# Three projection tiles behind the input loads, and the sum of squares split before the first eviction

## The chip, the cores and the metric

The kernel runs on one core of a Trainium2 chip. The metric is the device time of one execution in microseconds, the median of the runs. The engines are TensorE (PE, its weight loads PEld), VectorE (DVE), ScalarE (ACT) and GpSimd (POOL); SyncE (SP) issues nearly all loads, ScalarE's queue a few.

## The reference, cut to what matters

Two layers of a hybrid encoder work on 512 grid tokens and 16 meta tokens (528 columns) of width 1024. A layer takes an RMS norm of its input, one wide projection, global attention (GQA) on one part and windowed attention (NA) on another, gates both, merges them and adds an output projection.

```python
def hybrid_layer(x, norm_g, w_in, q_norm_g, k_norm_g, rpb, w_o_attn, w_o_na, w_out, cos, sin):
    h = rms_norm(x, norm_g)
    proj = jnp.einsum('bld,de->ble', h, w_in)
    qa, ka, va, za, qb, kb, vb, zb, ga, gb = split_cols(proj)
    qa = apply_axial_rope(rms_norm(qa.reshape(...), q_norm_g), cos, sin)
    ka = apply_axial_rope(rms_norm(ka.reshape(...), k_norm_g), cos, sin)
    oa = gqa_attention(qa, ka, va) * jax.nn.silu(za)
    ...
    mixed = jax.nn.sigmoid(ga) * ya + jax.nn.sigmoid(gb) * yb
    return x + jnp.einsum('bld,de->ble', mixed, w_out)
```

## The kernel before, in words

The input comes transposed, in eight feature tiles of 128 features x 528 tokens (264 KB each). A projection tile is 128 columns of w_in; layer 0 starts with QA to QA+3 (queries of the global attention), KA, VA, and then four times KB, QB, VB, ZB, ZA, followed by the gates GB and GA with the output halves y between them. A tile sums over eight k steps. For precision each operand is a high part (fp32r, made by ScalarE) and a low part (the difference, made by VectorE for the input, `normed`, and by GpSimd for the weights), and each k takes three products, for two token halves of 264 columns: 48 matmuls for a tile. The norm's gain is in the operands; the factor of each token (`rbc`) is applied when a later tile is evicted, and the per-head norm of q and k makes the first tiles independent of it.

**The head.** `piece` loads, casts and splits a quarter of the weights of QA or QA+1 (256 columns, two k), `half` a half (512 columns, four k), `feature` one feature tile. The tuple at line 403 sets their order; `in_order` queues each behind the last cast on ScalarE and GpSimd. Behind the last feature tile come the squares of three feature tiles and their adds, the weights of QA+2, and the rest of the squares, some of them behind the first evictions (`input_squares`, `sum_up`, `late`). The products of QA and QA+1 (line 429) follow the feature tiles: QA's sums lie in two banks of the pool `ps_p`, which all later tiles use too, those of QA+1 in the two banks of `S`. QA+2 is the first tile that `product` makes, with `weights` loading and splitting its halves in the list `order`.

**Evictions.** `rotated` empties each half of a tile with three ScalarE instructions (lines 470 to 472) and takes a low part on VectorE; `rotate` are four VectorE instructions, `stack_pair` makes the operand of the attention.

**Side work.** Each half of a `product` ends in a tick. Two queues, `side_gqa` and `side_na`, issue their due parts at ticks: `later(n, part)` is due n ticks on. The sum of the squares is split (`norm_split`), turned into factors (`norm_root`) and spread (`norm_spread`) at the ticks of `NORM_AT`. Attention units start at ticks whose count is a multiple of four (GQA) or one more (NA) and issue scores, transposes and sums some ticks on; `side_na.finish()` and `side_gqa.finish()` tick what is left, behind the third GB and the third GA tile. The products at line 434 have no ticks.

The scheduler orders each engine's instructions by priority (`high_priority`) and by when their inputs and buffers come free in its own reckoning; `issue_after` fixes an order on one engine. The slots of a tag are reused: "O" has 8, "K" 4, "E" 6, "G" 8.

Of the kernel before, what the change touches and what calls it, by code (L numbers as in the profile page):

```python
# [11 lines left out]
F32 = mybir.dt.float32  # L12
F32R = mybir.dt.float32r
I32 = mybir.dt.int32
AF = mybir.ActivationFunctionType
# [23 lines left out]
NA_AT = ({"stages": (0, 2, 5, 5, 5, 7), "values": (3, 4)},  # L39
         {"stages": (0, 2, 4, 5, 5, 7), "values": (3, 4)})  # L40

NORM_AT = ({"tokens": (1, 4, 6), "squares": (2, 2, 2, 3, 2), "heads": (2, 3, 5, 7, 6), "values": (1, 4)},
           {"tokens": (1, 3, 5), "squares": (2, 2, 2, 3, 2), "heads": (2, 3, 5, 7, 6), "values": (1, 4)})
GQA_AT_TICK, NA_AT_TICK = (0, 0), (1, 1)

# [50 lines left out]
def trunk_kernel(ctx: ExitStack, tc: tile.TileContext, xT, w, gn, gf, bias, rope, out):  # L96
# [28 lines left out]
    def bank(pool, name, tag):  # L125
        return pool.tile([P, 512], F32, tag=tag, name=name)
# [81 lines left out]
    for l in range(DEPTH):  # L208
        cols = [QA, QA + 1, QA + 2, QA + 3, KA, VA]
        for j in range(4):  # L210
            cols += [KB + j, QB + j, VB + j, ZB + j, ZA + j]
        order += [(l, c, i) for c in cols for i in range(2)]
        if l == 0:

            order = order[1:2] + order[3:]
        for gate, wo in ((GB, WOB), (GA, WOA)):
            for m in range(8 + LAG):
                order += [(l, gate + m, 0), (l, gate + m, 1)] if m < 8 else []
                order += [(l, wo + (m - LAG) // 2, (m - LAG) % 2)] if m >= LAG else []
        order += [(l, WOUT + m, i) for m in range(8) for i in range(2)] if l < DEPTH - 1 else []  # L220
# [107 lines left out]

    h_last = {}

    def normed(l, k, x, n):

        hi, lo = slot("h", f"hh{l}_{k}", F32R), slot("h", f"hl{l}_{k}", F32R)
        h_last["hi"] = nc.scalar.mul(hi[:, :n], x, g_in[l][:, k:k + 1])
        h_last["lo"] = nc.vector.scalar_tensor_tensor(lo[:, :n], x, g_in[l][:, k:k + 1], hi[:, :n].bitcast(F32),
                                                      op0=ALU.mult, op1=ALU.subtract)
        return hi, lo

    def squared(first, x, n, name):
        sq = slot("R" if first else "G", f"sq{name}")  # L340
        h_last["square"] = nc.scalar.activation(sq[:, :n], x, AF.Square)
        return sq
# [30 lines left out]


    pieces, xs, h, done = {}, [], [], [None, None]

    def in_order(part):
        with ExitStack() as held:
            for ins in done:
                if ins is not None:  # L380
                    held.enter_context(tc.issue_after(ins))
            part()

    def piece(c, i):
        raw = slot("K", f"rawp{c}_{i}")[:, :2 * P]
        hi, lo = (slot("O", f"w{'hl'[v]}p{c}_{i}", F32R)[:, :2 * P] for v in range(2))
        nc.sync.dma_start(raw, w[0, c][:, 2 * P * i:2 * P * (i + 1)])
        done[0] = nc.scalar.copy(hi, raw).ins
        done[1] = nc.gpsimd.tensor_sub(lo, raw, hi.bitcast(F32)).ins
        pieces[c, i] = hi, lo  # L390

    def half(c):
        weights(0, c, 1, 1)
        done[:] = split_at["weights"]

    def feature(k):
        if k % 2 == 0:
            xs.extend(two("M", f"x0_{k}"))
        nc.sync.dma_start(xs[k], xT[k])
        h.append(normed(0, k, xs[k], NTOK))  # L400
        done[0] = h_last["hi"].ins

    for part in ((piece, QA, 0), (feature, 0), (piece, QA + 1, 0), (feature, 1), (piece, QA, 1), (piece, QA + 1, 1),
                 (feature, 2), (feature, 3), (half, QA), (feature, 4), (half, QA + 1), (feature, 5), (feature, 6), (feature, 7)):
        in_order(lambda: part[0](*part[1:]))

    def input_squares(ks):
        return [squared(k == 0, xs[k], NTOK, f"0_{k}") for k in ks]

    def sum_up(sqs):  # L410
        for sq in sqs:
            nc.vector.tensor_add(total["ss"], total["ss"], sq)

    total, late = {}, []
    with tc.issue_after(h_last["hi"].ins), tc.issue_after(h_last["lo"].ins):
        total["ss"], *sqs = input_squares(range(3))
        sum_up(sqs)
    with tc.issue_after(h_last["square"].ins):
        weights(0, QA + 2, 1, 1)
    with tc.issue_after(split_at["weights"][0]):  # L420
        sum_up(input_squares((3, 4)))
        late.append(input_squares((5, 6)))


    first, ends = {}, ((0, HALF), (HALF, NTOK))
    for c, ps in ((QA, [bank(ps_p, f"pp0_{QA}_{a}", "pp")[:, :HALF] for a, _ in ends]),
                  (QA + 1, ps_s.tile([P, 2, 512], F32, tag="S", name=f"pp0_{QA + 1}"))):
        first[c] = [(ps[i] if c == QA else ps[:, i, :HALF], a, b) for i, (a, b) in enumerate(ends)]
    for c, k in sorted(((c, k) for c in first for k in range(KT)), key=lambda x: (x[1] + 2 * (x[0] > QA and x[1] > 3), x[0])):
        wh, wl = (t[:, P * (k % 4):P * (k % 4 + 1)] for t in weights(0, c, k // 4, 1)) if k > 3 else (  # L430
            t[:, P * (k % 2):P * (k % 2 + 1)] for t in pieces[c, k // 2])
        for wt, rt in ((wh, 0), (wh, 1), (wl, 0)):
            for ps, a, b in first[c]:
                nc.tensor.matmul(ps, wt, h[k][rt][:, a:b], start=k == 0 and wt is wh and rt == 0,
                                 stop=k == KT - 1 and wt is wl)

    for l in range(DEPTH):
        last = l == DEPTH - 1
# [21 lines left out]
        def rotated(c, g, full, name):  # L460

            n, j = NTOK if full else NREAL, c - QA

            if name == "k":
                keys.append(slot("KR", f"{name}{l}_{c}")[:, :NTOK + NMETA])
            q = slot("E", f"{name}{l}_{c}") if name == "q" else keys[0][:, NMETA:]
            sq = slot("G", f"{name}s{l}_{c}")
            qh, ql = slot("G", f"{name}h{l}_{c}", F32R), slot("G", f"{name}l{l}_{c}", F32R)
            for ps, a, b in project(c, full):
                nc.scalar.mul(q[:, a:b], ps, g)  # L470
                nc.scalar.activation(qh[:, a:b], ps, AF.Square)
                evac["last"] = nc.scalar.activation(sq[:, a:b], ps, AF.Square)  # L472
            with tc.high_priority():
                evac["low"] = nc.vector.tensor_sub(ql[:, :n], sq[:, :n], qh[:, :n].bitcast(F32))
            side_gqa.later(NORM_AT[l]["squares"][j], lambda: sum_squares(j, n, qh, ql))

            def rotate():
                sh = slot("G", f"{name}r{l}_{c}")
                nc.vector.stream_shuffle(sh[:, :n], q[:, :n], [(i + 16) % 32 for i in range(32)])
                nc.vector.tensor_mul(sh[:, :n], sh[:, :n], sin[:, :n])  # L480
                nc.vector.tensor_mul(q[:, :n], q[:, :n], cos[:, :n])
                nc.vector.tensor_add(q[:, :n], q[:, :n], sh[:, :n])

            return q, rotate
# [56 lines left out]
        st = {}  # L541

        def norm_split():
            st["ss"] = split_squares(total["ss"], NTOK, f"{l}")

        def norm_root():
            st["mx"], st["rx"], st["root"] = inverse_rms(st["ss"], NTOK, f"{l}")
# [24 lines left out]
        for j in range(4):  # L572
            q, rotate = rotated(QA + j, g_q[l], full, "q")
            qs.append(q)

            with tc.issue_after(evac["low"].ins):
                if l == 0 and j < 2:
                    sum_up(late[j])
                if l == 0 and j == 0:
                    turn = rotate  # L580
                    with tc.issue_after(evac["last"].ins):
                        late.append(input_squares((7,)))
                else:
                    if turn:
                        turn()
                    turn = None
                    rotate()
            if j > 1:
                stack_pair(j - 2)
            if j == 0:  # L590
                for after, part in zip(NORM_AT[l]["tokens"], (norm_split, norm_root, norm_spread)):
                    side_gqa.later(after, part)
                if full:
                    side_gqa.later(5, meta_columns)
        k, rotate = rotated(KA, g_k[l], True, "k")
        rotate()
        stack_pair(2)

        def pair_factors(t, c, n, name):

# [123 lines left out]

        v = scaled(VA, f"va{l}")
        with tc.issue_after(evac["v"].ins):
            stack_pair(3)
# [496 lines left out]
```

## Time and profile before

| what | us |
|---|---|
| median of 3 runs | 862.96 |
| lowest, highest | 862.93, 865.67 |
| profiled execution | 862.94 |
| its span, first to last instruction | 861.2 |
| TensorE busy | 849.1 |
| VectorE busy | 533.4 |
| ScalarE busy | 491.6 |
| GpSimd busy | 360.6 |

The span is what the profiler records of the core; the rest of the execution's time lies around it. Busy times are sums of records. Matmuls are pipelined, so their records overlap and short idle times of TensorE don't show in its busy time.

### The profile page before, as it was taken

How to read it: one execution, taken by the hardware profiler on the slowest of the kernel's cores; microseconds unless marked ns; L12 is line 12 of the kernel's file. 1: busy time of each engine (PE TensorE's matmuls, PEld its weight loads, DVE VectorE, ACT ScalarE, POOL GpSimd, SP SyncE). 2: the span in 40 equal slices, each digit the busy share in tenths (PEclk: the TensorE clock that was granted, in tenths of full speed). 3: DMA queues.
4: the chain of work that ended last, by engine and by line, in shares of the span. 5: the costliest groups of instructions: out<-in, count | busy, mean ns of one | idle time of the engine just before them, and what ended most of it. 6: DMA issues, size and time to landing. Idle time of an engine off the chain costs nothing. (4 is left out here: it accounts for less than half of the span.)

```text
span 861.2 us, 16238 instructions
## 1 busy us (share of the span) xinstructions
PE 849.1 (99%) x5960; PEld 788.7 (92%) x5960; DVE 533.4 (62%) x1309; ACT 491.6 (57%) x1178; POOL 360.6 (42%) x287
## 2 busy tenths in 40 slices
PE   8999999999999999999999999999999999999997
PEld 8999999999999999999998999999988888878786
DVE  6985767677774574436548656677767645444633
ACT  8644677576874564333445456578667655543422
POOL 5574233342232333454764653324333233334751
PEclk9999999999999999999999999999999999999999
DMA  6364344325112222325655664334532222223602
GB/s 237 104 190 132 98 118 113 115 64 163 50 50 75 74 74 63 104 84 155 150 137 130 171 172 136 103 98 131 146 103 74 75 75 78 93 79 98 206 22 98
DMA packets 64670, 95.55 MB, mean 111 GB/s; under 512 B 22864, under 2 KB 23376, under 8 KB 64592
## 3 DMA queue, kind: packets, MB, share of 16 engines
q1 hardware_dynamic: 63872, 93.46, 37.2%
q8 instruction: 47, 0.77, 0.4%
q10 hardware_dynamic: 720, 1.06, 0.3%
q14 instruction: 31, 0.25, 0.1%
HBM read 76.72 MB, written 4.19 MB: 94 GB/s over the span
## 5 line engine op out<-in xcount | busy, mean ns | idle before, releaser
L238 POOL TENSOR_TENSOR wlo<-raw,whi 128x512 fp32r<-128x512 f32 x214 | 285.2, 1337 | 453.0 <-ACT whi L237 377.5
L320 PE MATMUL pp<-hh,whi 128*128 128x264 f32 (+1 forms) x1056 | 334.8, 317 | 0.6 <-ACT qs L472 0.6
L322 PE MATMUL pp<-hh,wlo 128*128 128x264 f32 (+1 forms) x1056 | 329.3, 312 | 0.0
L321 PE MATMUL pp<-hl,whi 128*128 128x264 f32 (+1 forms) x1056 | 327.9, 310 | 0.0
L237 ACT CAST whi<-raw 128x512 fp32r<-128x512 f32 x214 | 131.4, 619 | 154.0 <-PE pp L321 57.4
L322 PEld LDWEIGHTS pp<-hh,wlo 128*128 128x128 f32 x1056 | 198.7, 188 | 10.8
L320 PEld LDWEIGHTS pp<-hh,whi 128*128 128x128 f32 x1056 | 198.8, 188 | 10.1 <-ACT qs L472 1.2
L321 PEld LDWEIGHTS pp<-hl,whi 128*128 128x128 f32 x1056 | 199.2, 189 | 9.1
L783 DVE CUSTOM_DVE_ANT_1 P<-S,r 128x528 f32<-128x528 f32 x64 | 45.1, 705 | 19.1 <-PE S L537 18.0
L194 DVE TENSOR_TENSOR ptl<-pt,pth 128x512 fp32r<-128x512 f32 x64 | 44.0, 689 | 17.5 <-ACT pth L193 16.9
L1048 DVE TENSOR_TENSOR mg<-pp,rbc 128x264 f32<-128x264 f32 (+1 forms) x48 | 24.8, 517 | 41.8 <-PE pp L322 41.4
L787 ACT ACTIVATE P<-P,st 128x528 f32<-128x528 f32 x64 | 47.2, 737 | 2.0
L908 ACT ACTIVATE bias<-bias,stb 128x208 f32<-128x208 f32 (+1 forms) x64 | 31.1, 486 | 24.1 <-DVE stb L906 23.8
L129 PE MATMUL pt<-ident,P 128*128 128x128 f32 x256 | 39.4, 275 | 1.3 <-DVE P L789 0.9
L193 ACT CAST pth<-pt 128x512 fp32r<-128x512 f32 x64 | 37.3, 584 | 4.3 <-PE pt L129 3.1
L1049 ACT ACTIVATE mg<-mg 128x264 f32<-128x264 f32 (+1 forms) x48 | 23.7, 493 | 25.9 <-DVE mg L1048 25.8
L321 PE MATMUL pp<-mx,whi 128*128 128x264 f32 x128 | 36.6, 286 | 0.0
L320 PE MATMUL pp<-mx,whi 128*128 128x264 f32 x128 | 36.4, 285 | 0.0
L322 PE MATMUL pp<-mx,wlo 128*128 128x264 f32 x128 | 36.3, 284 | 0.0
L830 PE MATMUL av<-pth,VA 128*128 128x256 f32 x128 | 35.3, 298 | 0.1
L789 DVE TENSOR_SCALAR P<-P,st 128x528 f32<-128x528 f32 x64 | 33.0, 516 | 2.1
L830 PE MATMUL av<-ptl,VA 128*128 128x256 f32 x128 | 33.0, 280 | 0.0
(529 smaller groups left out, 1749.3 us busy)
## 6 DMA issues: line engine op xcount, KB each, us to landing
raw<-in_w_dram SPq DMA_DIRECT2D x214, 256.0 KB, 2.7
bias<-in_bias_dram SPq DMA_DIRECT2D x16, 480.0 KB, 3.8
KB<-KB SPq DMA_DIRECT2D x24, 272.0 KB, 3.8
rawl<-in_w_dram SPq DMA_DIRECT2D x16, 256.0 KB, 3.0
x<-in_xT_dram SPq DMA_DIRECT2D x8, 264.0 KB, 4.3
xr<-in_xT_dram SPq DMA_DIRECT2D x8, 264.0 KB, 4.1
Q<-q SPq DMA_DIRECT2D x16, 128.0 KB, 3.2
x1d<-xt SPq DMA_DIRECT2D x32, 64.0 KB, 2.8
```

The costliest lines, as they stand in the source:

```text
L129: nc.tensor.transpose(ps, src, ident[:n, :n])
L193: split_at["hi"] = nc.scalar.copy(hi, src)
L194: split_at["any"] = nc.vector.tensor_sub(lo, src, hi.bitcast(F32))
L237: cast = nc.scalar.copy(hi, raw)
L238: sub = nc.gpsimd.tensor_sub(lo, raw, hi.bitcast(F32))
L320: nc.tensor.matmul(ps, wh, rh[:, a:b], start=i == 0, stop=False)
L321: nc.tensor.matmul(ps, wh, rl[:, a:b], start=False, stop=False)
L322: nc.tensor.matmul(ps, wl, rh[:, a:b], start=False, stop=i == n - 1)
L783: newest["max"] = nc.vector.tensor_tensor_reduce(p[:n].rearrange("p (i k) -> p i k", i=2), S[:n, :, :HALF], scale[:n].unsqueeze(2).to_broa ...
L787: nc.scalar.activation(p[:n], p[:n], AF.Exp, bias=st[:n, 1:2], scale=1.0, accum_out=st[:n, 2:3])
L789: nc.vector.tensor_scalar_mul(p[:n], p[:n], st[:n, 3:4])
L830: nc.tensor.matmul(c["av"], rows2(c["t"][i][0]), c["t"][i][1], start=i == 0, stop=i == 8)
```

## The change

Three tiles, QA, QA+1 and QA+2, follow the input. Their weights lie in memory as eight row tiles: row tile k holds the 384 columns of all three tiles for one k (192 KB). The head loads a row tile and a feature tile in turn. From k = 4 on the square of feature tile k - 4 and its add are put behind feature tile k; the other four, the first half of QA+3's weights and the split of the sum follow. The first feature tile's high part is made in two halves. QA+2's sums lie in the banks `avn` and `avg`, which the attention uses later. The products of k = 0 to 3 go through all three tiles, the later ones in a written order that ends QA first. Each half's evictions are queued behind the ones before. Numbers of ticks in `NORM_AT` and the places of `stack_pair` are edited, and `order` begins with QA+3.

```diff
-NORM_AT = ({"tokens": (1, 4, 6), "squares": (2, 2, 2, 3, 2), "heads": (2, 3, 5, 7, 6), "values": (1, 4)},
+NORM_AT = ({"tokens": (1, 1, 3), "squares": (1, 1, 2, 3, 2), "heads": (2, 3, 5, 7, 6), "values": (1, 4)},
...
-            order = order[1:2] + order[3:]
+            order = order[6:]
...
+    w3 = w[0, QA:QA + 3].rearrange("c p n -> (c p n)").rearrange("(k p n) -> k p n", k=KT, p=P)
...
-    def piece(c, i):
-        raw = slot("K", f"rawp{c}_{i}")[:, :2 * P]
-        hi, lo = (slot("O", f"w{'hl'[v]}p{c}_{i}", F32R)[:, :2 * P] for v in range(2))
-        nc.sync.dma_start(raw, w[0, c][:, 2 * P * i:2 * P * (i + 1)])
+    def row_tile(k):
+        raw = slot("K" if k < 4 else "E", f"rawp{k}")[:, :3 * P]
+        in_turn(raw, w3[k])
+        hi, lo = (slot("O", f"w{'hl'[v]}p{k}", F32R)[:, :3 * P] for v in range(2))
         done[0] = nc.scalar.copy(hi, raw).ins
         done[1] = nc.gpsimd.tensor_sub(lo, raw, hi.bitcast(F32)).ins
-        pieces[c, i] = hi, lo
+        pieces[k] = hi, lo
...
     def feature(k):
...
-        nc.sync.dma_start(xs[k], xT[k])
-        h.append(normed(0, k, xs[k], NTOK))
+        in_turn(xs[k], xT[k])
+        h.append(normed(0, k, xs[k], NTOK, ((0, HALF), (HALF, NTOK)) if k == 0 else None))
         done[0] = h_last["hi"].ins
...
+    def add_up(k):
+        sq = square(k)
+        if k == 0:
+            total["ss"] = sq
+        else:
             nc.vector.tensor_add(total["ss"], total["ss"], sq)
...
+    def next_weights():
+        weights(0, QA + 3, 0, 1)
+        done[:] = split_at["weights"]
+
+    def sum_split():
+        total["split"] = split_squares(total["ss"], NTOK, "0")
+        done[0] = split_at["hi"].ins
+
+    for k in range(KT):
+        in_order(lambda: row_tile(k))
+        in_order(lambda: feature(k))
+        if k > 3:
+            in_order(lambda: add_up(k - 4))
+    for k in range(4, KT):
+        in_order(lambda: add_up(k))
+    in_order(next_weights)
+    in_order(sum_split)
...
+                  (QA + 2, [bank(ps_a, f"pp0_{QA + 2}_{tag}", tag)[:, :HALF] for tag in ("avn", "avg")])):
...
+    def first_products(c, k):
+        wh, wl = (t[:, P * (c - QA):P * (c - QA + 1)] for t in pieces[k])
+        for wt, rt in ((wh, 0), (wl, 0), (wh, 1)):
             for ps, a, b in first[c]:
...
+    for k in range(4):
+        for c in range(QA, QA + 3):
+            first_products(c, k)
+    for c, k in ((0, 4), (1, 4), (0, 5), (1, 5), (0, 6), (2, 4), (0, 7), (1, 6), (1, 7), (2, 5), (2, 6), (2, 7)):
+        first_products(QA + c, k)
...
-                nc.scalar.mul(q[:, a:b], ps, g)
-                nc.scalar.activation(qh[:, a:b], ps, AF.Square)
-                evac["last"] = nc.scalar.activation(sq[:, a:b], ps, AF.Square)
+                with ExitStack() as held:
+                    if "last" in evac:
+                        held.enter_context(tc.issue_after(evac["last"].ins))
+                    nc.scalar.mul(q[:, a:b], ps, g)
+                    nc.scalar.activation(qh[:, a:b], ps, AF.Square)
+                    evac["last"] = nc.scalar.activation(sq[:, a:b], ps, AF.Square)
...
-            st["ss"] = split_squares(total["ss"], NTOK, f"{l}")
+            st["ss"] = total.pop("split", None) or split_squares(total["ss"], NTOK, f"{l}")
...
-            if j > 1:
-                stack_pair(j - 2)
+            if j > 1 + (l == 0):
+                stack_pair(j - 2 - (l == 0))
...
-                    side_gqa.later(5, meta_columns)
+                    side_gqa.later(4, meta_columns)
...
+    w[0, QA:QA + 3] = w_in[0][:, :3 * P].reshape(3, P, KT * P)
```

## Rows read from the trace of the kernel before

**Rows 1.** The page's part 1: busy us (share of the span) xinstructions.
```profile
PE 849.1 (99%) x5960; PEld 788.7 (92%) x5960; DVE 533.4 (62%) x1309; ACT 491.6 (57%) x1178; POOL 360.6 (42%) x287
```
**Rows 2.** Waits of TensorE, whole span: us in total, times, longest.
```profile
PE pt L129 <- DVE P L789: 0.9, 1, 0.9
```
**Rows 3.** Timeline of TensorE, head: start, us, instructions, [idle before <-releaser].
```profile
1.11 4.39 PE L137 MATMUL warm<-zero 128*128 128x128 f32 x20 [1.11 <-DVE one L143]
...
5.25 0.48 PE L434 MATMUL pp<-hh,whp 128*128 128x264 f32 x2
5.84 0.51 PE L434 MATMUL pp<-hl,whp 128*128 128x264 f32 x2
...
9.43 0.51 PE L434 MATMUL pp<-hl,whp 128*128 128x264 f32 x2 [0.28 <-DVE hl L335]
...
13.55 0.51 PE L434 MATMUL pp<-hl,whi 128*128 128x264 f32 x2 [0.31 <-DVE hl L335]
13.90 0.40 PE L434 MATMUL pp<-hh,wlo 128*128 128x264 f32 x2
...
18.29 0.40 PE L434 MATMUL pp<-hh,wlo 128*128 128x264 f32 x2
19.24 0.39 PE L320 MATMUL pp<-hh,whi 128*128 128x264 f32 x1 [0.56 <-ACT qs L472]
...
25.20 0.28 PE L455 MATMUL mh<-qh,means_r 128*10 128x264 f32 x1
```
**Rows 4.** Stretches of the head: busy per engine, then PEclk, DMA share, GB/s.
```profile
6.00:10.00 4.00, 3.72 (x29) 3.51 (x30) 2.47 (x3) 3.68 (x7) 2.47 (x4) 1.00 0.98 344
10.00:14.00 4.00, 3.69 (x30) 3.47 (x29) 3.23 (x4) 3.57 (x7) 2.71 (x2) 1.00 1.04 402
```
**Rows 5.** Timeline of ScalarE, head.
```profile
11.43 2.06 ACT L334 ACTIVATE hh<-x,gains 128x528 fp32r<-128x528 f32 x3
...
15.00 1.12 ACT L237 CAST whi<-raw 128x512 fp32r<-128x512 f32 x2
16.03 2.24 ACT L341 ACTIVATE sq<-x 128x528 f32<-128x528 f32 x4
18.18 0.46 ACT L470 ACTIVATE q<-pp,gains 128x264 f32<-128x264 f32 x1
...
19.09 0.47 ACT L470 ACTIVATE q<-pp,gains 128x264 f32<-128x264 f32 x1
```
**Rows 6.** Timeline of VectorE, head.
```profile
5.02 0.77 DVE L335 SCALAR_TENSOR_TENSOR hl<-x,gains,hh 128x528 fp32r<-128x528 f32 x1 [2.65 <-ACT hh L334]
...
16.70 3.02 DVE L412 TENSOR_TENSOR sq<-sq,sq 128x528 f32<-128x528 f32 x2 [0.42 <-ACT sq L341]
...
31.44 0.70 DVE L482 TENSOR_TENSOR q<-q,qr 128x528 f32<-128x528 f32 x1
32.06 0.70 DVE L481 TENSOR_TENSOR q<-q,cos 128x528 f32<-128x528 f32 x1
```
**Rows 7.** Timeline of GpSimd, head.
```profile
3.54 0.74 POOL L389 TENSOR_TENSOR wlp<-rawp,whp 128x256 fp32r<-128x256 f32 x1 [1.56 <-ACT whp L388]
...
15.68 3.48 POOL L238 TENSOR_TENSOR wlo<-raw,whi 128x512 fp32r<-128x512 f32 x2 [2.75 <-ACT whi L237]
```
**Rows 8.** The tile raw to 40 us: durations in ns, minimum/median/maximum, first and last start.
```profile
L238 POOL TENSOR_TENSOR wlo<-raw,whi x10: 1286/1526/1770, 9.7 to 38.9; 128x512 fp32r<-128x512 f32 x10
```
**Rows 9.** Timeline of TensorE, the first attention unit.
```profile
72.29 0.55 PE L129 MATMUL pt<-ident,P 128*128 128x128 f32 x3 [0.90 <-DVE P L789]
```
**Rows 10.** Timelines of VectorE and TensorE, the two ends of layer 0's attention.
```profile
255.30 0.69 DVE L194 TENSOR_TENSOR ob<-ob,ob 128x528 fp32r<-128x528 f32 x1
...
258.32 0.28 PE L320 MATMUL y<-ob,whi 128*128 128x264 f32 x1
...
347.21 0.71 DVE L194 TENSOR_TENSOR oa_3b<-oa,oa_3a 128x528 fp32r<-128x528 f32 x1 [0.70 <-ACT oa_3a L193]
...
351.37 0.28 PE L320 MATMUL y<-oa_3a,whi 128*128 128x264 f32 x1
```

More of the change, by code (lines that the diff above doesn't have):

```diff
@@ L329, in trunk_kernel, with normed @@
     h_last = {}
-    def normed(l, k, x, n):
+    def normed(l, k, x, n, spans=None):
         hi, lo = slot("h", f"hh{l}_{k}", F32R), slot("h", f"hl{l}_{k}", F32R)
-        h_last["hi"] = nc.scalar.mul(hi[:, :n], x, g_in[l][:, k:k + 1])
+        for a, b in spans or ((0, n),):
+            h_last["hi"] = nc.scalar.mul(hi[:, a:b], x[:, a:b], g_in[l][:, k:k + 1])
         h_last["lo"] = nc.vector.scalar_tensor_tensor(lo[:, :n], x, g_in[l][:, k:k + 1], hi[:, :n].bitcast(F32),
@@ L382, in in_order @@
             part()
-    def piece(c, i):
-        raw = slot("K", f"rawp{c}_{i}")[:, :2 * P]
-        hi, lo = (slot("O", f"w{'hl'[v]}p{c}_{i}", F32R)[:, :2 * P] for v in range(2))
-        nc.sync.dma_start(raw, w[0, c][:, 2 * P * i:2 * P * (i + 1)])
+    def row_tile(k):
+        raw = slot("K" if k < 4 else "E", f"rawp{k}")[:, :3 * P]
+        in_turn(raw, w3[k])
+        hi, lo = (slot("O", f"w{'hl'[v]}p{k}", F32R)[:, :3 * P] for v in range(2))
         done[0] = nc.scalar.copy(hi, raw).ins
         done[1] = nc.gpsimd.tensor_sub(lo, raw, hi.bitcast(F32)).ins
-        pieces[c, i] = hi, lo
-    def half(c):
-        weights(0, c, 1, 1)
-        done[:] = split_at["weights"]
+        pieces[k] = hi, lo
     def feature(k):
@@ L398, in feature @@
             xs.extend(two("M", f"x0_{k}"))
-        nc.sync.dma_start(xs[k], xT[k])
-        h.append(normed(0, k, xs[k], NTOK))
+        in_turn(xs[k], xT[k])
+        h.append(normed(0, k, xs[k], NTOK, ((0, HALF), (HALF, NTOK)) if k == 0 else None))
         done[0] = h_last["hi"].ins
-    for part in ((piece, QA, 0), (feature, 0), (piece, QA + 1, 0), (feature, 1), (piece, QA, 1), (piece, QA + 1, 1),
-                 (feature, 2), (feature, 3), (half, QA), (feature, 4), (half, QA + 1), (feature, 5), (feature, 6), (feature, 7)):
-        in_order(lambda: part[0](*part[1:]))
@@ L407, in input_squares @@
[L407 to L411, printed above, removed]
-            nc.vector.tensor_add(total["ss"], total["ss"], sq)
[L414 to L422, printed above, removed]
+    total = {}
@@ new lines, in square @@
+    def square(k):
+        sq = squared(k == 0, xs[k], NTOK, f"0_{k}")
+        done[0] = h_last["square"].ins
+        return sq
+    def add_up(k):
[3 more added lines that the diff above has]
+        else:
+            nc.vector.tensor_add(total["ss"], total["ss"], sq)
+    def next_weights():
[4 more added lines that the diff above has]
+        done[0] = split_at["hi"].ins
@@ L425, in trunk_kernel @@
+    for k in range(KT):
[7 more added lines that the diff above has]
+    in_order(sum_split)
     first, ends = {}, ((0, HALF), (HALF, NTOK))
+    two_banks = ps_s.tile([P, 2, 512], F32, tag="S", name=f"pp0_{QA + 1}")
     for c, ps in ((QA, [bank(ps_p, f"pp0_{QA}_{a}", "pp")[:, :HALF] for a, _ in ends]),
-                  (QA + 1, ps_s.tile([P, 2, 512], F32, tag="S", name=f"pp0_{QA + 1}"))):
@@ L428, in trunk_kernel @@
[L428 to L432, printed above, removed]
+                  (QA + 1, [two_banks[:, i, :HALF] for i in range(2)]),
@@ L433, in trunk_kernel @@
+                  (QA + 2, [bank(ps_a, f"pp0_{QA + 2}_{tag}", tag)[:, :HALF] for tag in ("avn", "avg")])):
+        first[c] = [(ps[i], a, b) for i, (a, b) in enumerate(ends)]
+    def first_products(c, k):
+        wh, wl = (t[:, P * (c - QA):P * (c - QA + 1)] for t in pieces[k])
+        for wt, rt in ((wh, 0), (wl, 0), (wh, 1)):
             for ps, a, b in first[c]:
                 nc.tensor.matmul(ps, wt, h[k][rt][:, a:b], start=k == 0 and wt is wh and rt == 0,
-                                 stop=k == KT - 1 and wt is wl)
+                                 stop=k == KT - 1 and rt == 1)
@@ L576, in trunk_kernel @@
             with tc.issue_after(evac["low"].ins):
-                if l == 0 and j < 2:
-                    sum_up(late[j])
                 if l == 0 and j == 0:
                     turn = rotate
-                    with tc.issue_after(evac["last"].ins):
-                        late.append(input_squares((7,)))
                 else:
@@ L593, in trunk_kernel @@
                 if full:
-                    side_gqa.later(5, meta_columns)
+                    side_gqa.later(4, meta_columns)
         k, rotate = rotated(KA, g_k[l], True, "k")
         rotate()
-        stack_pair(2)
+        stack_pair(2 - (l == 0))
         def pair_factors(t, c, n, name):
@@ L726, in trunk_kernel @@
         with tc.issue_after(evac["v"].ins):
-            stack_pair(3)
+            for j in range(3 - (l == 0), 4):
+                stack_pair(j)
         VA2 = tiny.tile([P, 5, 2, 2, HD], F32R, tag="VA2", bufs=1, name=f"VA2{l}")
```

## The prediction

> **What bounds the kernel now.** First the busy times: TensorE is busy in 849.1 of 861.2 us, the next engine in 533.4 [rows 1]. So only two things can move the end: fewer columns on TensorE, or fewer stretches in which it stands. The change keeps every product, so I look for stretches. The waits of TensorE over the whole span name few; the longest is 0.9 us [rows 2]. Because matmuls overlap in their records, an idle time under some 0.16 us doesn't show there; the start times do better. In the head, 36 matmuls of 264 columns start from 13.90 to 18.29 us, 0.122 us each [rows 3]. The first three projection tiles are 3 x 48 = 144 such matmuls, 17.57 us at that pace. They take from 5.25 to 25.20 us, 19.95 us [rows 3]. The lost 2.4 us lie ahead of four starts: at 5.84, 9.43 and 13.55 us VectorE's low part of the input was late (two rows name it), and at 19.24 us it was the bank of QA, which ScalarE began to empty only behind seven squares [rows 3, 5]. The granted clock is 1.00 in this stretch [rows 4], so the clock gives nothing back.
>
> **Start.** The first real matmul starts at 5.25 us, right where the 20 warm-up matmuls end, which run from 1.11 us on (5.50 us by their modelled end) [rows 3]. Cutting the first high part in two halves (one ScalarE instruction more) can't start TensorE earlier, since the warm-up is kept. The low part of tile 0 still needs both halves. It ended at 5.79 us [rows 6]; I leave it there. With the new order four products instead of two stand ahead of it, to 5.74 us. Left of that wait: 0.1 us, and 0.1 us at which the pace picks up. So of the 2.4 us about 2.2 can go.
>
> **The input as a source.** A feature tile (264 KB) and its row tile (192 KB) are 467,000 bytes. At 344 to 402 GB/s [rows 4] a pair lands every 1.2 to 1.4 us. Three tiles take from each pair 18 matmuls, 2.2 us; two tiles took 12, 1.5 us. This is the real content of the change: more products per byte landed, so TensorE should run behind the loads with a growing lead of data. Without a further wait the three tiles end at 5.84 + 140 x 0.122 + 0.1 = 23.0 us, where they now end at 25.2. SP issues 16 loads as before and no more bytes: the third tile's weights come earlier, QA+3's later.
>
> **ScalarE.** Casts: 4 of 256 and 4 of 512 columns become 8 of 384, the same columns. A cast of 512 costs 0.56 us, so 384 about 0.42 (an estimate, by columns); a high part 0.66 to 0.69, a square 0.56 [rows 5]. Eight of each are 13.2 us; from the first load at 4.25 us they end at 17.5 or later. QA is complete on TensorE after 114 matmuls, at 19.3 us. So the squares no longer stand ahead of the eviction of QA, if nothing else holds ScalarE. Three instructions empty bank a in 0.91 us [rows 5]: free at 20.2 us, wanted at 23.0. The wait ahead of 19.24 us goes. A new wait: row tiles 4 to 7 reuse the eight O buffers, so the last cast waits for TensorE to finish k = 3 at 14.1 us, and the high part 7 and the squares are queued behind it. At 1.1 to 1.6 us per k ScalarE gets there at about that time: 0.
>
> **VectorE and GpSimd.** This is where I expect something back. Alone, instructions of VectorE follow each other in 0.62 us, and a low part on GpSimd takes 0.74 us for 256 columns and 1.29 for 512 [rows 6 to 8]; 384 columns lie between, 1.0 by columns. But from 15.68 to 19.72 us two low parts took 3.48 us, where 2.58 would do, and two adds 3.02 us, where 1.24 would do: 3.8 us of work in 4.04 us [rows 6, 7]. They went one after the other. The head now has 8 low parts of the input, 7 adds and 8 low parts of weights: 15 x 0.62 + 8 x 1.0 = 17.4 us in one line. It starts at about 3.75 us and waits some 1.0 us for the first loads: 22.2 us. Then the split of the sum, 0.56 us, and, if it stands ahead of the first eviction on ScalarE, bank a of QA is free at 23.6 us instead of 23.0: 0.6 us of waiting for the first matmul of QA+3. If they could run side by side, the last add would end at 18.1 us and the cost would be 0. If low part 7 is late instead (19.7 us, wanted at 19.0), that is the same 0.6 to 0.7 us, not a second one. Bounds 0 and 3.2 (the low parts of both halves of QA+3 ahead of the adds, 2.6 us more in the line); I take 0.6, the sum by the pace of the rows.
>
> The Trainium skill ("SBUF — State Buffer", section "Who interferes with whom") says that a VectorE instruction with two inputs in SBUF contends with a GpSimd instruction that reads SBUF, and that the second to issue "fully blocks". By that rule the whole line above is serial and costs the 0.6 us; by the view that engines with their own queues run side by side it costs nothing. The trace agrees with the rule: 3.8 us of work in 4.04.
>
> **The side work.** QA+2 no longer ticks the side queues, so every later tick falls two product halves earlier in count. The edited lists keep the norm and the heads where they stood against the products or earlier. GQA units start on multiples of four: the first stays at tick 12, which is now behind VB 0 and not behind QB 0, two product halves later. The 0.9 us that TensorE lost ahead of 72.29 us, where the second set of scores of unit 0 wasn't scaled yet on a crowded VectorE [rows 9], then has other work around it. Bounds: a loss as large, and a gain of all 0.9. I take a gain of 0.5.
>
> The price comes at the end of layer 0: the last windowed head and the last GQA unit finish two halves (5.9 us) later against the products. Before, the windowed output was ready at 255.99 us and the tenth matmul of y, which first reads it, at 259.4; the GQA output at 347.92, read at 351.37 [rows 10]: 3.4 us of cover each. At most 2.5 us are lost at each place. The loops that finish the queues issue what is left without waiting for ticks, which gives up to two halves back: 0. I take 0.2 in all. Layer 1 keeps its phases, since the last units end at the same ticks (56 and 87).
>
> **Sum.** -2.2 + 0.6 - 0.5 + 0.2 = -1.9 us. The profiled execution took 862.94 us (span 861.2, 1.7 around it), the median of the runs is 862.96. Forecast 861.0 us, with its own range 860.2 to 862.0.
>
> **Rivals.**
> More than forecast: the line of VectorE and GpSimd leaves gaps that cost nothing, and the wait ahead of 72.29 us goes whole: -2.2 - 0.9 = -3.1, 859.8 us. For it: QA+2 and QA+1 stand between QA's end and the next need of its bank (3.7 us). Against: the serial rows.
> No gain: the low part of QA+3's first half (1.29 us) also gets ahead of the adds. The sum is then ready at 23.4, split at 24.0, bank a free at 24.9: 1.9 of 2.2 us are back as a wait of another name, 862.6 us. For it: GpSimd held its ground in the row at 15.68, where it lost 0.9 us and VectorE 1.8.
> Slower: ScalarE works in order, and the split of the sum stands ahead of all evictions and of the casts of QA+3's second half. Add both halves' low parts (2.6 us) to the line: split at 25.3, bank a at 26.2, 3.2 us late. If the second half's cast stands behind the evictions of QA and QA+1 (1.82 us each), its low part is ready at 30.8, wanted at 27.8: 3.0 more. 6.2 - 2.2 = +4.0: 866.9 us; without the last step 863.9. It costs from an end of the adds at 21.5 us on, and it is slower than before from 23.7 on. Against: casts were put between evictions before.
> The change doing less than it says: the halves of the first high part, which start nothing earlier; that is in the forecast.
>
> **Chances.** Forecast 0.52, more 0.20, no gain 0.18, slower 0.10. A measurement tells 0.3%, 2.6 us, from no change. Faster by more: the second case and the forecast's low edge, 0.25. Slower by more: the heavier part of the last case, 0.06. Between: 0.69. Range: from 859.2, below the second case, to 863.6, above the third; the slow case is left out.
>
> **What would show it.** Right: TensorE without a wait over 0.2 us from 5.84 us to the first matmul of QA+3 at 23.0 to 23.7 us; the last add at 21 to 22.5 us; adds and low parts of weights longer than alone. Wrong: a wait for the low part of the input at k = 1 to 6 (the loads or the line are slower than worked out); the last add before 19.5 us (no serial line); waits of TensorE over 1 us at 250 to 260 or 340 to 352 us (the drains cost); a start before 5.2 us.

## The result, and the profile after

The changed kernel takes 865.6 us (median of 17 runs, 864.67 to 867.33), the kernel before 863.2 us (17 runs): ratio 1.0025, interval 1.0018 to 1.0032. It is slower by 2.4 us, outside the range. The profiled executions differ by 2.0 us: 864.96 us (span 863.2) against 862.94 us (span 861.2). Of the 17 runs the five with a mean granted clock of 0.999, the profiled one among them, took 864.67 to 865.08 us, and the one at 0.994 took 867.33 us.

The page's part 1 answers to [rows 1]: TensorE is busy 1.2 us less in a span 2.0 us longer. So time went into standing.

```profile
PE 847.9 (98%) x5960; PEld 787.9 (91%) x5960; DVE 535.3 (62%) x1309; ACT 489.8 (57%) x1179; POOL 363.0 (42%) x287
```

The waits of TensorE (us in total, times, longest) answer to [rows 2], and say where. The 0.9 us behind VectorE's P are gone. Two larger waits are new, and three smaller ones (the last three lines).

```profile
PE pp L320 <- ACT qs L492: 2.7, 1, 2.7
PE Sm L556 <- DVE st L800: 1.3, 1, 1.3
...
PE pt L129 <- DVE VB L194: 0.7, 1, 0.7
...
PE ta L129 <- issue: 0.5, 1, 0.5
PE tb L129 <- DVE mm L958: 0.4, 1, 0.4
```

The head of TensorE's timeline (start, us, instructions, idle before) answers to [rows 3]. The last matmul of the three tiles starts at 23.38 us, so they end at 23.5, where they ended at 25.20. Then TensorE stands until 26.32. What the change won, 1.7 us, is lost again and 1.1 us more.

```profile
1.11 4.14 PE L137 MATMUL warm<-zero 128*128 128x128 f32 x20 [1.11 <-DVE one L143]
5.01 0.95 PE L445 MATMUL pp<-hh,whp 128*128 128x264 f32 x4
...
7.38 0.28 PE L445 MATMUL pp_avg<-hl,whp 128*128 128x264 f32 x1
7.77 0.51 PE L445 MATMUL pp<-hh,whp 128*128 128x264 f32 x2
8.12 0.41 PE L445 MATMUL pp<-hh,wlp 128*128 128x264 f32 x2
8.57 0.51 PE L445 MATMUL pp<-hl,whp 128*128 128x264 f32 x2
...
23.38 0.28 PE L445 MATMUL pp_avg<-hl,whp 128*128 128x264 f32 x1
26.32 0.39 PE L320 MATMUL pp<-hh,whi 128*128 128x264 f32 x1 [2.66 <-ACT qs L492]
```

The loads came as fast as before [rows 4]: 392 and 387 GB/s, the granted clock 1.00 (columns as there).

```profile
6.00:10.00 4.00, 3.85 (x29) 3.42 (x28) 1.87 (x3) 3.45 (x7) 2.83 (x3) 1.00 1.05 392
10.00:14.00 4.00, 4.00 (x35) 4.00 (x34) 3.89 (x3) 3.99 (x9) 3.92 (x4) 1.00 1.05 387
```

ScalarE, VectorE and GpSimd in the head answer to [rows 5 to 7]. Read them together. ScalarE has started to empty bank a of QA at 20.09 us; its next instruction is the high part of the sum (ssh), for which it stands 4.51 us. VectorE's last five adds run from 18.41 to 25.04 us. From 19.22 to 24.47 us GpSimd makes three low parts of the next weights, both halves of QA+3 and the first of KA: ScalarE had cast all three ahead of the first eviction.

```profile
15.86 2.77 ACT L342 ACTIVATE sq<-x 128x528 f32<-128x528 f32 x5
18.54 1.65 ACT L237 CAST whi<-raw 128x512 fp32r<-128x512 f32 x3
20.09 0.47 ACT L490 ACTIVATE q<-pp,gains 128x264 f32<-128x264 f32 x1
25.07 0.63 ACT L193 CAST ssh<-sq 128x528 fp32r<-128x528 f32 x1 [4.51 <-DVE sq L413]
25.61 0.38 ACT L491 ACTIVATE qh<-pp 128x264 fp32r<-128x264 f32 x1
25.89 0.38 ACT L492 ACTIVATE qs<-pp 128x264 f32<-128x264 f32 x1
```
```profile
18.41 6.63 DVE L413 TENSOR_TENSOR sq<-sq,sq 128x528 f32<-128x528 f32 x5
25.73 0.71 DVE L194 TENSOR_TENSOR ssl<-sq,ssh 128x528 fp32r<-128x528 f32 x1 [0.70 <-ACT ssh L193]
```
```profile
19.22 5.25 POOL L238 TENSOR_TENSOR wlo<-raw,whi 128x512 fp32r<-128x512 f32 x3 [2.60 <-ACT whi L237]
```

Two stretches of the attention show the side work (window: length, TensorE busy, clock, DMA share, GB/s), first the kernel before, then the changed one. The wait of [rows 9] lay in the first stretch and is gone. In the second 0.4 us were idle; now it is 3.4 us.

```profile
60.00:80.00 20.00, 19.09 (x157) 1.00 0.68 182
170.00:260.00 90.00, 89.59 (x738) 1.00 0.28 81
```
```profile
60.00:80.00 20.00, 19.98 (x166) 1.00 0.69 191
170.00:260.00 90.00, 86.64 (x715) 1.00 0.29 81
```

The first matmul that turns the heads' sums (mt) starts 0.8 us later than before (51.06 against 50.29), the first of layer 0's output product (on mx) 2.2 us later (399.45 against 397.25); layer 1 adds nothing. At the two ends of [rows 10], the first matmul on ob starts at 259.31 us (258.32 before), that on oa at 352.74 (350.28), and neither waits itself. But the longest wait of the second stretch lies right ahead of that on ob, at a score of the attention:

```profile
258.77 0.33 PE L556 MATMUL Sm<-KA0h,Q2m 128*64 128x264 f32 x1 [1.35 <-DVE st L800]
```

### The profile page after: what moved, and what is told of

Its sections match the earlier page's. It is cut to its first block, busy times and chain, and to the rows that moved or that the text cites. A ratio compares the mean times of both kernels' runs of the same rounds, so it can differ in the third digit from the quotient of the medians.

```text
span 863.2 us, 16235 instructions
## 1 busy us (share of the span) xinstructions
PE 847.9 (98%) x5960; PEld 787.9 (91%) x5960; DVE 535.3 (62%) x1309; ACT 489.8 (57%) x1179; POOL 363.0 (42%) x287
## 5 line engine op out<-in xcount | busy, mean ns | idle before, releaser
L238 POOL TENSOR_TENSOR wlo<-raw,whi 128x512 fp32r<-128x512 f32 x210 | 280.7, 1340 | 445.7 <-ACT whi L237 374.4
L320 PE MATMUL pp<-hh,whi 128*128 128x264 f32 (+1 forms) x1040 | 329.7, 317 | 2.7 <-ACT qs L492 2.7
L322 PE MATMUL pp<-hh,wlo 128*128 128x264 f32 (+1 forms) x1040 | 324.3, 312 | 0.0
L321 PE MATMUL pp<-hl,whi 128*128 128x264 f32 (+1 forms) x1040 | 323.6, 311 | 0.0
L237 ACT CAST whi<-raw 128x512 fp32r<-128x512 f32 x210 | 129.1, 619 | 154.9 <-PE pp L321 55.3
L320 PEld LDWEIGHTS pp<-hh,whi 128*128 128x128 f32 x1040 | 195.7, 188 | 11.8 <-ACT qs L492 2.9
L322 PEld LDWEIGHTS pp<-hh,wlo 128*128 128x128 f32 x1040 | 195.7, 188 | 10.7
L321 PEld LDWEIGHTS pp<-hl,whi 128*128 128x128 f32 x1040 | 196.2, 189 | 9.1
L1066 ACT ACTIVATE mg<-mg 128x264 f32<-128x264 f32 (+1 forms) x48 | 23.5, 492 | 21.3 <-DVE mg L1065 21.0
```

The lines of the kernel that those rows point to most:

```text
L237: cast = nc.scalar.copy(hi, raw)
L238: sub = nc.gpsimd.tensor_sub(lo, raw, hi.bitcast(F32))
L320: nc.tensor.matmul(ps, wh, rh[:, a:b], start=i == 0, stop=False)
L321: nc.tensor.matmul(ps, wh, rl[:, a:b], start=False, stop=False)
L322: nc.tensor.matmul(ps, wl, rh[:, a:b], start=False, stop=i == n - 1)
```

## Experiments

Times are medians; a ratio is to the kernel before, run beside it. Two causes are on trial: the wait ahead of QA+3, and the ticks of the side work. For the first there are two explanations: that low parts on GpSimd stretch VectorE's adds, or that ScalarE's order alone is to blame, whatever the adds take. The expectations name their theories A and B anew for each run.

**The split of the sum behind the evictions (e1_split_late).**

```
-    in_order(sum_split)
...
+            if l == 0 and j == 2:
+                with tc.issue_after(evac["last"].ins):
+                    total["split"] = split_squares(total["ss"], NTOK, "0")
```

> The split of the sum stands behind the evictions of QA to QA+2 on ScalarE, nothing else is edited. Theory A: of the 2.8 us that TensorE waits ahead of QA+3 (23.4 to 26.3 us), all comes from the split, which holds ScalarE from 20.5 to 25.1 us until the last add is done. Then QA+3 starts at 23.5 to 23.7 us and the kernel takes 865.6 - 2.7 = 862.9 us; what is lost later in layer 0 stays. Rival B: ScalarE would be late without the split as well, or the low part of QA+3's weights is what comes last: QA+3 still starts after 25 us and the time stays within 1 us of 865.6.

Measured: 868.4 us, ratio 1.0048 (1.0032 to 1.0063). QA+3 no longer waits for its bank, but the norm's matmuls wait 1.2 us for ssh, and the low parts of QA's and QA+1's squares, which stand behind the adds on VectorE, hold up ScalarE for 2.2 us. The adds themselves take 7.89 us here, beside four low parts on GpSimd. Then a cost that no expectation held: after these waits the granted clock falls from 1.00 (2.4 GHz) to 0.50 (1.2 GHz) and stays there from about 30.5 to 41 us. TensorE starts 11 matmuls in 2 us there, where it started 19.

```profile
24.00:26.00 2.00, 2.00 (x19) 1.00 0.52 167
28.00:30.00 2.00, 1.11 (x9) 1.00 0.10 39
30.00:32.00 2.00, 1.66 (x8) 0.63 0.02 4
32.00:34.00 2.00, 2.00 (x11) 0.50 0.01 4
...
38.00:40.00 2.00, 2.00 (x11) 0.50 0.00 0
40.00:42.00 2.00, 2.00 (x16) 0.81 0.32 72
```

Neither theory held: the wait ahead of QA+3 went, and the time rose. So the order on ScalarE is not the whole cause: moving the split moves the wait.

**The ticks as before (e2_ticks).** Two ticks at QA+2, and due times two later.

```
-"tokens": (1, 1, 3), "squares": (1, 1, 2, 3, 2)
+"tokens": (3, 3, 5), "squares": (3, 3, 2, 3, 2)
...
+                if l == 0 and c == QA + 2:
+                    tick()
...
-                    side_gqa.later(4, meta_columns)
+                    side_gqa.later(6 if l == 0 else 4, meta_columns)
```

> The third tile's evictions tick the side queues again (two ticks), and the due times of the head are raised by two, so that the head's side work keeps its place and the attention units get back the places they had before the change. The split of the sum stays ahead of the evictions. Theory A: the head is the same (QA+3 at 26.3 us), and of the 2.0 to 2.4 us some 1.2 come from the two halves by which units start later against the products (waits at 173, 182, 247 and 257 us): these go, 864.4 us. Rival B: these waits follow from the head's delay, not from the ticks: 865.6 us, with waits over 0.8 us left between 160 and 260 us.

Measured: 863.82 us, ratio 1.0005 (0.9996 to 1.0013): 1.8 us below the changed kernel. The wait for the bank stays (2.77 us). The waits at 170 to 260 us are gone. The wait near 73 us is back (1.25 us, 0.90 in the kernel before), and one of 0.5 us near 61 us is there that neither kernel has.

```profile
60.00:80.00 20.00, 18.24 (x149) 1.00 0.68 181
170.00:260.00 90.00, 89.60 (x739) 1.00 0.27 79
```

So the moved ticks cost, where the forecast had them gain. Later pairs of runs that differ by the ticks alone say 1.5, 1.6 and 0.6 us (e4 and e8, e12 and e13, e6 and e7). A fifth pair, e1 and e3, says 3.7, but there the stretch of low clock differs, too.

**Both (e3_both).** The two edits above together.

> Both edits: the split behind the evictions and the two ticks back. Theory A: both gains add up, 865.6 - 2.7 - 1.2 = 861.7 us, 1.5 us below the kernel before. Rival B (head alone matters, later waits are chance): 862.9 us, as with the split alone.

Measured: 864.73 us, ratio 1.0015 (1.0007 to 1.0024). The norm's matmuls wait 1.2 us for ssh and 1.0 for ssl, and the clock falls to 0.50 near 37 us. The adds take 7.89 us here, too. The time is neither A's 861.7 nor B's 862.9: the two edits don't add up.

**No low parts beside the adds (e4_memset).** This kernel leaves three low parts out and writes zeros for them. The order of instructions is the changed kernel's on every engine.

```
-            sub = nc.gpsimd.tensor_sub(lo, raw, hi.bitcast(F32))
+            sub = nc.gpsimd.memset(lo.bitcast(F32), 0.0) if len(ready) < 3 else nc.gpsimd.tensor_sub(lo, raw, hi.bitcast(F32))
```

> The low parts of the first three halves of weights behind the head (both of QA+3, the first of KA) are left out: GpSimd writes zeros in their place, which reads nothing; all engines keep the order of their instructions. Theory A: the last five adds on VectorE took 6.6 us instead of 3.2 because the three low parts on GpSimd ran between them. Now they end near 21.6 us, the split near 22.3, and QA+3 starts at 23.5 to 23.7 us: 862.9 us. Rival B: the adds are late for another reason (their squares, or GpSimd being busy at all): they still end after 24 us and the time stays at 865.6.

Measured: 862.69 us, ratio 0.9989 (0.9981 to 0.9998), 2.9 us below the changed kernel. In the timelines of VectorE and of ScalarE the same five adds take 3.94 us, and the split starts at 22.50; GpSimd had written its zeros from 16.68 to 18.13 us. TensorE starts QA+3 without a wait, with the split where the change put it. So this run's theory A holds, and ScalarE's order is not too late in itself. As the zeros were written ahead of the adds, the run doesn't tell GpSimd's reading beside them from its work of any kind.

```profile
18.52 3.94 DVE L413 TENSOR_TENSOR sq<-sq,sq 128x528 f32<-128x528 f32 x5
```
```profile
22.50 0.64 ACT L193 CAST ssh<-sq 128x528 fp32r<-128x528 f32 x1 [1.72 <-DVE sq L413]
```

**One low part ahead of the adds, two behind (e6_early), and with the ticks (e7_early_ticks).**

```
+    in_order(next_weights)
     for k in range(4, KT):
         in_order(lambda: add_up(k))
-    in_order(next_weights)
...
+                    if l == 0 and c == QA and a == 0:
+                        total["behind"] = evac["last"].ins
+                        weights(0, QA + 3, 1, 1)
+                        evac["last"] = split_at["cast"]
```

The cast of the third half is held behind the same eviction.

> The changed kernel, but of the weights that follow the three tiles only the first half is cast ahead of the squares, so that its low part runs on GpSimd before most of the adds; the second half is cast right behind the eviction of the first bank, the third behind it. Nothing is left out. Theory A (low parts on GpSimd slow VectorE's adds, 6.63 us for five against 3.94 without them): the five adds take 3.9 to 4.5 us, the split of the sum starts by 22.9, TensorE idles under 0.8 us ahead of QA+3 (2.66 in the changed kernel), time 865.6 - 2.3 = 863.3. Rival B (the cast of the sum stands ahead of the evictions and is too late whatever the adds take, the zeros of the earlier run having saved something else): adds over 5.5 us or idle time over 1.5 us, time 864.6 to 865.6.

> The same edit, and the ticks of side work put back as they were in the kernel before (one at QA+2, the due times of the norm and of the squares' sums two later). Nothing is left out. If the two causes are separate and add up: 863.3 - 1.8 = 861.5, faster than both kernels. Rival: the ticks gave 1.8 us only because the late head had shifted the side work; with an early head the waits near 61 and 72 us come back (0.8 and 1.4 us in the run with ticks alone) and the time is 862.7 to 863.3.

Measured: 864.94 us, ratio 1.0020 (1.0011 to 1.0029), and with the ticks 864.32, ratio 1.0011 (1.0003 to 1.0020). The adds do take 3.94 us, but start 0.75 us later: the one low part now runs beside the low part of the input, which takes 1.80 us instead of 0.76 (VectorE, then GpSimd). The wait for the bank is 0.9 us, and sums of squares wait 0.6 more. The adds came as A had them; the times lie in B's range (864.6 to 865.6) and above both of the second expectation's. The first low part was paid at another instruction of VectorE.

```profile
17.43 1.80 DVE L339 SCALAR_TENSOR_TENSOR hl<-x,gains,hh 128x528 fp32r<-128x528 f32 x1
19.16 3.94 DVE L416 TENSOR_TENSOR sq<-sq,sq 128x528 f32<-128x528 f32 x5
```
```profile
16.99 1.68 POOL L241 TENSOR_TENSOR wlo<-raw,whi 128x512 fp32r<-128x512 f32 x1 [0.66 <-ACT whi L240]
```

**No low parts, and the ticks (e8_memset_ticks).** The edits of e4_memset and e2_ticks.

> The low parts of the first three halves of weights behind the three tiles are left out (zeros written by GpSimd in their place), and the ticks of side work are put back. If the two causes add up: 862.7 - 1.8 = 860.9. Rival (the ticks are worth nothing once the head has no wait): 862.7.

Measured: 861.14 us, ratio 0.9975 (0.9965 to 0.9984). The two causes are separate: 2.7 to 2.9 us for the low parts, 1.5 to 1.8 for the ticks. With both gone the kernel is about 2 us below the kernel before, near the 2.2 us that the forecast gave the head. The loss between 170 and 260 us goes with the ticks, whatever the head does: TensorE is busy 86.63 of these 90 us in e4_memset, 89.58 here.

**Late split with later due times (e9_late_due).** e3_both with tokens (5, 5, 6) and squares (4, 4, 2, 3, 2).

> The run with the late split and the ticks of the kernel before (864.7 us), with three due times later: the root of the norm two ticks (a matmul waited 1.4 us for the high part and 1.2 us for the low part of the split there, 0.7 us for the root's spread), the spread one tick, the sums of the squares of QA and QA+1 one tick (0.45 us). Nothing is left out. If those waits, and the stretch near 36 us at the lower of TensorE's two clocks that followed them, are what kept that run from its gain: waits of 3.8 us and some 2 us of half clock go, less what the side work brings later; the granted clock stays 1.00 from 20 to 45 us, time 861.0 (860 to 862), below both kernels. Rival (VectorE's line of adds, low parts and rotations is the limit, so the wait moves on to the next reader): the same 3 to 4 us of idle time stand elsewhere before 60 us, time 863.5 to 865.

Measured: 866.15 us, ratio 1.0026 (1.0015 to 1.0037). The rival's case, and worse than its 863.5 to 865 us: one wait of 3.1 us on the low part of squares, and the clock at 0.50 from about 33 to 40 us. The adds take 7.87 us. Later due times moved the waits into one.

**The three tiles alone (e10_tiles_alone), and with the spread of the root behind KA (e11_spread_later).** Squares summed as before, ticks as before.

```
-    for k in range(4, KT):
-        in_order(lambda: add_up(k))
+    in_order(lambda: add_up(4))
+    late = []
+    in_order(lambda: late.append([square(5), square(6)]))
     in_order(next_weights)
-    in_order(sum_split)
```

The last square and the adds of these three stand in the loop over QA, as in the kernel before. The second run adds one order, that of the transposes of norm_spread behind the last product traced.

> The first part of the change alone: three feature tiles follow the input, row tiles of weights as in the changed kernel; but the squares are summed as in the kernel before (the sum up to the fifth square ahead of the evictions, two adds behind the low part of QA's squares, the last behind that of QA+1's, the split where side work calls it), and the ticks are those of the kernel before with the sums of the heads' squares one tick later. Nothing is left out. If the early sum and split are what turns the change's gain into a loss: QA+3 starts within 0.5 us of the end of the three tiles (2.66 us of idle time in the changed kernel), no wait over 0.8 us follows up to 45 us, and the time is 861.3 (860.5 to 862), 2 us below the kernel before, like the run with zeros and ticks (861.1). Rival (VectorE's line up to 30 us holds too much once three tiles end together, whatever its order; the late-split runs speak for it): 1.5 us or more of idle time between 23 and 37 us on sums of squares or norm factors, time 863 to 864.5.

> The run with three tiles alone (867.2 us), with one order changed: the matmuls that spread the norm's root over the partitions stand behind the products of KA, where the kernel before has them, and not ahead of them, where TensorE waited 5.4 us for GpSimd's root and fell to the lower of its two clocks for some 9 us. Nothing is left out. If that one wait is all that kept the three tiles alone from their gain: no wait over 0.8 us from 20 to 60 us, the clock 1.00 throughout, and 867.2 - 5.4 - about 4.5 of half clock + up to 4 for what was hidden behind it = 861.3 (860.5 to 862.3), below both kernels. Rival (VectorE's and GpSimd's lines are too long after three tiles that end together): the wait comes back at another reader, 1.5 us or more before 60 us, time 863 to 865.

Measured: 867.17 us, ratio 1.0037 (1.0024 to 1.0051). QA+3 doesn't wait, but the spread of the root stands ahead of KA and waits 5.2 us, and the clock is at 0.50 from about 33 to 43 us. GpSimd's root stood there behind two low parts (5.63 us from 29.78). The time lies above the expected range and the rival's. With that order changed: 863.91 us, ratio 1.0006 (0.9997 to 1.0015), in the rival's range; the profiled execution is the fastest of the 11, at 862.82. Waits of 0.4 us on squares and 1.4 on KA's bank are left, and mt starts at 50.28 us, as before (50.29). The two waits of TensorE:

```profile
PE rb L580 <- POOL rx L204: 5.2, 1, 5.2
```
```profile
PE pp L320 <- ACT qs L492: 1.4, 1, 1.4
...
PE mh L472 <- DVE ql L496: 0.4, 1, 0.4
```

So the early sum alone is not what spoils the change: under the kernel before's own order of sums the shorter head is given back, too. Ahead of the longer wait ScalarE stands for two instructions of VectorE that take 1.77 and 1.78 us (from 30.12 and 31.82 us), beside two low parts of weights on GpSimd; 0.70 us is their time alone. That these low parts cause the wait wasn't tried.

**The low parts on VectorE, behind its adds (e12_vector_low, e13_vector_low_ticks).**

```
+                if len(ready) < 3:
+                    held.enter_context(tc.issue_after(total["added"]))
+                sub = (nc.vector if len(ready) < 3 else nc.gpsimd).tensor_sub(lo, raw, hi.bitcast(F32))
...
-            nc.vector.tensor_add(total["ss"], total["ss"], sq)
+            total["added"] = nc.vector.tensor_add(total["ss"], total["ss"], sq).ins
```

> The changed kernel, but the low parts of the first three halves of weights behind the three tiles are made by VectorE, behind its last add of squares, and not by GpSimd beside the adds. Nothing is left out; VectorE gets three instructions of some 0.62 us more. If it is GpSimd running beside VectorE that stretches the adds (and not the adds themselves): five adds 3.94 us as in the run with zeros, split at 22.5, first low part done by 23.1 and second by 23.8, so no wait over 0.5 us ahead of QA+3 or in it, time 862.8 (the run with zeros had 862.7). Rival (VectorE's line is too long by the added 1.9 us): a wait of 1 us or more on low parts, on sums of squares or on ms up to 35 us, time 864 to 865.

> The same, with the ticks of side work of the kernel before (as in the other runs with ticks). Nothing is left out. If both causes are mended: 861.2 (the run with zeros and ticks had 861.1), 2.1 us below the kernel before and 4.4 below the changed one, the wait for the bank of QA+3 under 0.5 us. Rival as beside: 862.8 to 863.6.

Measured: 862.57 us, ratio 0.9989 (0.9980 to 0.9998), and with the ticks 861.0 us, ratio 0.9970 (0.9958 to 0.9982), below both kernels. Nothing is left out in them. VectorE does more, and is done earlier: the low parts that took 5.25 us on GpSimd take 1.29 us for two and 0.68 for the third, and the adds are whole again. TensorE goes from the last matmul of the three tiles to QA+3 at its pace (VectorE, then TensorE, of the run with ticks).

```profile
17.93 3.95 DVE L416 TENSOR_TENSOR sq<-sq,sq 128x528 f32<-128x528 f32 x5
21.79 1.29 DVE L241 TENSOR_TENSOR wlo<-raw,whi 128x512 fp32r<-128x512 f32 x2
23.00 0.70 DVE L194 TENSOR_TENSOR ssl<-sq,ssh 128x528 fp32r<-128x528 f32 x1
23.62 0.68 DVE L241 TENSOR_TENSOR wlo<-raw,whi 128x512 fp32r<-128x512 f32 x1
```
```profile
23.43 0.28 PE L448 MATMUL pp_avg<-hl,whp 128*128 128x264 f32 x1
23.55 0.28 PE L323 MATMUL pp<-hh,whi 128*128 128x264 f32 x1
```

Between 170 and 260 us the first run still has the loss of the moved ticks, the second has not:

```profile
170.00:260.00 90.00, 86.57 (x716) 1.00 0.28 84
170.00:260.00 90.00, 89.58 (x739) 1.00 0.28 83
```

## Why the prediction was wrong

**The head of TensorE (-2.2): right in kind, 0.5 us too large.** The waits of [rows 3] went. Two are left at the second pair of loads, 0.27 and 0.21 us beyond the pace (7.38 to 7.77 and 8.12 to 8.57 us). The second is ahead of the input's low part, one of the signs that I had named for an error. The three tiles end at 23.5 us, not 23.0. The start at 5.01 us is another such sign; but the warm-up itself was 0.25 us shorter (4.14 against 4.39 us), and other runs with the same head start between 4.89 and 5.40 us, so this says nothing of the halved high part.

**VectorE and GpSimd (+0.6): the step that failed.** Its mechanism held: adds and low parts of weights hold each other up. Its size didn't: the wait was 2.8 us, near the bound of 3.2 that I gave and did not take. Two things in it were off, and a third is easily misread.

First, which low parts stand in the line. I took none of the next weights and bounded by two; there were three, since ScalarE, done with the squares at 18.6 us, had 1.5 us ahead of the first eviction and cast three halves. The prediction saw that ScalarE would be free and didn't ask what it would do with that. Taking these out alone gave 2.9 us (e4_memset), putting them on VectorE gave 3.0 (e12_vector_low). Without them the last add ended at 22.46 us (e4_memset), where the prediction had 22.2; with them at 25.04. So the rest of the line came out nearly as summed, and what was missing was these three.

Second, the adds. I had them at 0.62 us, the spacing of [rows 6] at 31.44 us. These five add into one tile, each reading what the one before wrote: 3.94 us, 0.81 from start to start, with nothing beside them. That is 0.8 us more than I had, so that e4_memset met the 22.2 us is luck in part. In the changed kernel only the first two of these spacings show, 0.4 us in all.

Third, how the line is to be summed. These are the first low part and the third add, then the second low part and the fourth add (GpSimd, then VectorE, each time):

```profile
19.22 1.84 POOL L238 TENSOR_TENSOR wlo<-raw,whi 128x512 fp32r<-128x512 f32 x1 [2.60 <-ACT whi L237]
20.02 1.60 DVE L413 TENSOR_TENSOR sq<-sq,sq 128x528 f32<-128x528 f32 x1
21.02 1.76 POOL L238 TENSOR_TENSOR wlo<-raw,whi 128x512 fp32r<-128x512 f32 x1
21.73 1.62 DVE L413 TENSOR_TENSOR sq<-sq,sq 128x528 f32<-128x528 f32 x1
```

The last three adds and the three low parts take turns, one after the other, as the prediction had it: the third add ends 0.56 us after the first low part, the second low part 1.16 us after that add. A record that starts while the other engine is at work holds its wait, too. Five adds (3.94 us) and three low parts (3 x 1.29, [rows 8]) would be 7.8 us; they took 6.63, since the spacings between adds and 0.1 to 0.2 us of each record lie under the other engine's work. The page "SBUF — State Buffer" of the Trainium skill, section "Who interferes with whom", has contention between these two kinds of instruction; its section "Summary: rules for kernel authors" has the second of them to issue blocked until the first is done. These rows agree with both.

**The split ahead of the evictions: the rival was right.** "Slower" had the split done at 25.3 us and the bank free at 26.2, without its last step 863.9 us. Measured: the split runs from 25.07 to about 25.6, the bank is free at 26.27. That the numbers agree so well is partly luck: the rival counted two low parts at 1.29 us, 2.6 in all, where three ran and lengthened the adds by 2.7; and it counted three instructions of the eviction behind the split, where two were left, as the first had run at 20.09. It got 0.10, for "casts were put between evictions before". They weren't put there now, and as the second half's cast was early, its last step (3.0 us) didn't happen. Its place was worked out and its price was near; its weight was wrong.

**The side work (-0.3 in all): wrong in sign.** The wait of [rows 9] went, a gain of 0.9 us as hoped at most. Part of this was the late head's doing: with the same ticks and no late head that wait is 0.5 us (e4_memset) and 0.8 us (e12_vector_low). And between 170 and 260 us TensorE now idles 3.4 us instead of 0.4. The prediction looked for the price only in the output products at the two ends of [rows 10], where the cover held. The price lies in attention units whose matmuls now come before VectorE's tiles st, VB and mm are there; the longest of these waits, 1.35 us ahead of 258.77, meets the sign that the prediction had named (over 1 us at 250 to 260 us), though at a score and not at the output product. Putting the ticks back gave 1.8, 1.5, 1.6 and 0.6 us in four pairs of runs. Which of the due times does it wasn't tried apart.

By the measured terms the profiled execution adds up so: -1.7 + 2.8 is +1.1 at QA+3; mt is 0.8 late, as one wait of the kernel before near 33 us is gone (0.36 us between two starts, at 33.43 and 33.79 us); the side work brings the output product to 2.2 late; 2.0 at the end. The median moved by 0.4 us more than the profiled executions did; where that lies no trace of this kernel shows.

## What to carry to other kernels

When a change frees an in-order engine, ask what it will do with the free time: here it cast ahead, which put GpSimd to work beside VectorE just where VectorE was awaited. A subtraction moved from GpSimd onto the busy VectorE can make VectorE's line shorter, where the two engines' instructions take turns, as they did here. And where a schedule counts ticks, a tick taken out moves everything behind it: put back the count, then look at all of the layer, not at its end.

## What the runs showed that I had not expected

- Three low parts of 128 x 512 took 5.25 us on GpSimd beside adds, their waits included, and 1.97 us on VectorE behind them (1.29 for two, 0.68 for one).
- Adds into one tile follow each other in 0.81 us, independent instructions of that size in 0.62. That each add reads the one before is the likely reason; no run varied it alone.
- TensorE's clock fell to half for 3 to 10 us after several short waits close together (e1_split_late and e3_both, the longest 1.23 us) or one of 3.1 or 5.2 us (e9_late_due, e10_tiles_alone). It did not fall in the profiled execution of the changed kernel, with one wait of 2.7 us, nor in that of e11_spread_later, with 1.4 and 0.4. Such waits can so cost more than their sum: by an estimate from the windows of e1_split_late its 10 us at half clock are worth some 4 us, as 11 matmuls start in 2 us instead of 19. Why the clock fell in one case and not in the other wasn't tried.
